# A hybrid Fourier and Hyena encoder layer on one core: another order of the Fourier phase, and first parts before second parts in the products

## The chip, the cores and the metric

The kernel runs on one core of one Trainium2 chip. The metric is the device time of one execution in microseconds (us), the median over several runs. A core has five engines with queues of their own: TensorE (PE, matrix products into PSUM), VectorE (DVE), ScalarE (ACT), GpSimd (POOL) and SyncE (SP, which only issues transfers here). ScalarE and GpSimd can issue transfers too. Each engine works through its instructions in the order in which the program holds them, and waits at the first whose inputs or buffers are not ready.

## The reference

Two sequences (called batches 0 and 1 here) of 1024 tokens by 1024 channels, in f32, go through the same layer:

```python
xn = rmsnorm(x, g_pre)
p = xn @ w_in
fv, fg, hv, hg, mg = split(p)                       # widths 1024, 1024, 3072, 1024, 2048
fz = fft over tokens and over groups of 256 channels of fv, real part
y_f = (fz * silu(fg)) @ w_fourier_out
v, x1, x2 = split(short_conv(hv, w_short))          # depthwise, width 3
kf = hyena_filters(...)                             # sin(w2 . sin(w1 . z)) @ w3, times exp decay, normalised, rfft
z = v
for n, gate in enumerate((x1, x2)):
    z = gate * long_conv(z, kf[:, n], hyena_d[n])   # FFT of length 2048, both directions
y_h = (z * silu(hg)) @ w_hyena_out
g_f, g_h = split(sigmoid(mg + b_merge))
out = (g_f * y_f + g_h * y_h) @ w_out
return x + rmsnorm(out, g_post)
```

## The kernel before

All large products run in a 32-bit format in which TensorE rounds its inputs (fp32r). To keep f32 accuracy each operand is split into a rounded first part h and a remainder l: `split` casts on ScalarE (L171) and subtracts on VectorE or GpSimd (L181). A product is then three matmuls, h by h, h by l and l by h; `mm3` issues them one after the other, and every matmul goes through one line (L194).

The work has four phases: `phase_fourier` (0 to about 226 us), `phase_main` (filters, input projections and long convolutions, to about 1720), `phase_gates` (to about 1924) and `phase_out`.

`phase_fourier` does for each batch the row norms, the scaled transposition of x, the projection to fv and the two-dimensional Fourier transform:

- `hidden(0)` makes the first layer of the filter network: two matmuls (phd), a range reduction in seven VectorE instructions each (`sin_of`), two Sin activations on ScalarE and a store. `hidden(1)` makes the second layer; it stands at the end of the phase.
- `norm(b)` loads the eight row tiles of x (128 tokens by 1024), squares each on ScalarE with a sum along the row (L320), computes the reciprocal roots in two groups of four tiles (`rstd`, L242 to L253, a chain of short VectorE instructions), and scales the identity by them into the diagonals dg (L325). For batch 1 the whole of it is pinned behind the last weight cast of half 1 (`behind`).
- `xtile(b, k)` multiplies blocks of x by the diagonals on TensorE (tpx), which transposes and normalises at once; ScalarE copies them out to xg (L344, two buffers, tag "xg", which the squares share); SP writes xg to DRAM (d_x, L345); VectorE and GpSimd form even and odd sums eo, which are split into eh and el. Token 512 is handled alone: two VectorE instructions of 128 by 2 elements for each k put its parts into `x5` (L173 and L181 in the profile).
- `weights(half, k)` loads 128 rows of the fv weights (wfv), forms sums wer and differences wor, and splits them into we and wo.
- `pfv` multiplies eh and el by the weights over eight k. In half (0, 0), six tiles are begun while the k come in, four in the four projection banks of PSUM (tag "mm") and two in banks with the tag "X". The sums of token 512 (p5, written pfx in the profile) are in an "X" bank.
- `fourier_half(b, half)` evicts the tiles as EE and OO, and runs the transform over tokens (`stage`: pse, pso, copied as sev, combined as sst, split as pp and qp) and over channels (pP, pQ), and stores fz. Its order is halves (0, 0), (0, 1), (1, 1), (1, 0).

The instructions are not in source order: a planner places them by its own costs when the kernel is built, subject to their dependencies. `tc.issue_after(i)` pins what is issued inside it behind instruction i, and `keep_in_program_order` ties one instruction. So a change of dependencies or pins also moves instructions that it does not name.

In the later phases `inproj` holds 128 by 512 weight parts h and l in two buffers each, makes them from a 256 KB load (wr: ScalarE casts wh, GpSimd subtracts wl) and multiplies them with all of xh and xl (pin). `forward` and `conv_back` are the transforms of the long convolution (pX, pT), `times` the products of the gates and of the output (pg, po), `project` those with w_fourier_out and w_hyena_out (pyf, pyh). All issue the three matmuls of a product in sequence:

```python
for n in range(2):
    for kk in range(4):
        k = 4 * q + kk
        s = slice(512 * n, 512 * n + 512)
        self.mm3(ps[:, s], (h[:, kk], l[:, kk]), (self.xh[k][:, s], self.xl[k][:, s]), k == 0, k == 7)
```

Of the kernel before, what the change touches and what calls it, by code (L numbers as in the profile page):

```python
# [16 lines left out]
P = 128  # L17
# [144 lines left out]
class K:  # L162
# [93 lines left out]
    def sin_of(self, y, k, out, src_ps, f, b):  # L256
# [14 lines left out]
        nc.scalar.activation(out, y, AF.Sin)  # L271

    def hidden(self, layer, px, pf):
# [14 lines left out]
        else:  # L288
# [5 lines left out]
            y, k = [[t[:, 0:512], t[:, 512:1024]] for t in (y, k)]  # L294
        for n in range(2):
            p = self.psum("mm", 4, "phd")
            nc.tensor.matmul(p, w, z[:, 512 * n:512 * n + 512], start=True, stop=True)
            self.sin_of(y[n], k[n], out[n], p, self.hfb[:, 2 * layer:2 * layer + 1],
                        self.hfb[:, 2 * layer + 1:2 * layer + 2])
        nc.sync.dma_start(self.d_h if layer else self.d_h1, h)  # L300


    def norm(self, b, px, pf):
# [3 lines left out]
        nc, a = self.nc, self.a  # L307
# [4 lines left out]
        for m in range(8):  # L312
# [4 lines left out]
            nc.sync.dma_start(x, a[f"x{b}"][m * P:(m + 1) * P, :])  # L317
            self.xs.append(x)
            sq = px.tile([P, D], F32, tag="xg", name="sq", bufs=2)
            nc.scalar.activation(sq, x, AF.Square, accum_out=ss[:, m:m + 1])  # L320
            if m % 4 == 3:
                q = slice(m - 3, m + 1)
                self.rstd(px, rs[:, q], ss[:, q], 4)
                for j in range(m - 3, m + 1):
                    nc.vector.tensor_scalar(dg[:, j], self.ident, rs[:, j:j + 1], None, op0=MUL)  # L325

    def xtile(self, b, k, px, fo):
# [11 lines left out]
        for n in range(2):  # L339
# [4 lines left out]
            nc.scalar.activation(xg[:, 512 * n:512 * n + 512], tp, AF.Copy, scale=self.gpre[:, k:k + 1])  # L344
        nc.sync.dma_start(self.d_x[b][k], xg[:, 0:L])  # L345
# [6 lines left out]
        x5 = fo["x5"][:, k]  # L352
        self.split(x5[:, b:b + 33:32], x5[:, 2 + b:35 + b:32], xg[:, 512:513].to_broadcast([P, 2]), "dve", "dve")
# [6 lines left out]
    def weights(self, pw, W, half, k, first):  # L360

        nc, a = self.nc, self.a
        w = pw.tile([P, 2, 2, 130], F32, tag="wfv", name="wfv", bufs=2)
        nc.sync.dma_start(w.rearrange("p a b c -> p (a b c)"), a["w_fv"][k * P:(k + 1) * P, half])
# [4 lines left out]
        for r, t in ((we, W[0]), (wo, W[1])):  # L369
            self.split(t[0][:, k], t[1][:, k], r.rearrange("p a b -> p (a b)"), "pool" if r is wo and not first else "dve", "act")  # L370
# [12 lines left out]
    def fourier_half(self, b, half, W, fo, px, pf, begun={}):  # L383
# [102 lines left out]
    def phase_fourier(self):  # L486
        tc, nc, a = self.tc, self.nc, self.a
        with ExitStack() as es:
# [7 lines left out]
            fo["x5"] = pc.tile([P, 8, 36], F32R, name="x5")  # L496
            fo["x5t"] = pc.tile([P, 260], F32R, name="x5t")
# [11 lines left out]
            for b in range(NB):  # L509
                fo["eh"] = pe.tile([P, 8, 2, 2, 256], F32R, tag="eh", name="eh")  # L510
                fo["el"] = pe.tile([P, 8, 2, 2, 256], F32R, tag="el", name="el")
                if b == 0:
                    self.hidden(0, px, pf)
                with tc.issue_after(behind.ins) if b else ExitStack():
                    self.norm(b, px, pf)
                begun = {}
                if b == 0:
                    W = self.open_weights(pw)
                    for e, m in [(0, 0), (0, 1), (0, 2), (0, 3), (1, 0), (1, 1)]:
                        begun[e, m] = self.psum("X", 2, "pfv1") if e else self.psum("mm", 4, "pfv0")  # L520
                for k in range(8):
                    if b == 0:
                        self.weights(pw, W, 0, k, True)
                    self.xtile(b, k, px, fo)
                    for (e, m), p in begun.items():
                        self.pfv(p, e, m, k, W, fo)
                for half in ((0, 1), (1, 0))[b]:
                    if b + half == 0:
# [936 lines left out]
```

## Time and profile before

| | |
|---|---|
| runs | 2443.44 to 2447.43 us, median 2446.82 |
| the profiled execution | 2449.26 us, its span 2447.1 us |
| granted TensorE clock, mean | 0.997 |
| TensorE | 2396.1 us busy, 13196 matmul records |
| VectorE, ScalarE, GpSimd | 1893.8, 1096.8 and 485.9 us busy |
| chain that ended last | PE 88%, DMA 5%, issue 3%, DVE 2% |

The names in the rows are those of the program with buffer numbers left out; `L194 PE MATMUL pin<-xh,wl` is the matmul of line 194 that writes pin from xh and wl. Behind a row of the groups stand the busy time, the mean duration of one in ns, the idle time of the engine just before them and what ended it. In a timeline row the start and the duration come first, and the idle time before it and its releaser stand in brackets. Matmuls overlap, so that the mean duration of one (392 ns for 512 columns) is longer than the distance between two.

### The profile page before, as it was taken

The page shows a single profiled execution, that of the slowest core. Times are in us where ns is not written, and L with a number is a line of the kernel's source. Part 1 is how long each engine was busy: PE and PEld are TensorE (multiplying, and loading weights), DVE is VectorE, ACT ScalarE, POOL GpSimd, SP SyncE. Part 2 cuts the span into 40 slices and gives each one's busy share as a digit, 9 for nine tenths or more (in the row PEclk, how much of TensorE's full clock was granted, in tenths as well). Part 3 has the DMA queues.
Part 4 walks back from the last instruction along what each step waited for, and adds up shares of the span by engine and source line. Part 5 has one row for each costly group of instructions (what it writes and reads, how often), then busy time and mean ns, then how long its engine had stood idle before and what let it go on. Part 6 is the DMA issues. An engine that isn't in the chain of part 4 may idle for free.

```text
span 2447.1 us, 36853 instructions
## 1 busy us (share of the span) xinstructions
PE 2396.1 (98%) x13196; PEld 2082.3 (85%) x13196; DVE 1893.8 (77%) x3405; ACT 1096.8 (45%) x2063; POOL 485.9 (20%) x516
## 2 busy tenths in 40 slices
PE   6999999999999999999999999999999999999998
PEld 5988888888888888888888888888788888888886
DVE  7687888888748999999989999766555455665677
ACT  5545677767633433334223333333344444544343
POOL 1341222222143433331000000112200111122111
PEclk9999999999999999999999999999999999999999
DMA  7545655555555555445434444335454567776543
GB/s 273 170 141 191 224 175 173 167 175 167 173 194 177 172 177 173 165 165 192 146 128 134 141 141 138 121 121 184 154 174 159 198 210 255 245 250 213 169 164 129
DMA packets 225151, 429.36 MB, mean 175 GB/s; under 512 B 23542, under 2 KB 87255, under 8 KB 224456
## 3 DMA queue, kind: packets, MB, share of 16 engines
q1 hardware_dynamic: 198444, 333.34, 41.1%
q0 software_dynamic: 26336, 93.65, 10.9%
q8 instruction: 104, 1.70, 0.3%
q14 instruction: 79, 0.65, 0.1%
q10 hardware_dynamic: 188, 0.02, 0.0%
HBM read 290.60 MB, written 136.31 MB: 174 GB/s over the span
## 4 chain that ended last, share of the span: by engine, by line
PE 88%; DMA 5%; issue 3%; DVE 2%; ACT 1%; POOL 1%; SPq 0%; DVEq 0%; POOLq 0%; ACTq 0%
PE pin L194 41%; PE pT L194 7%; PE pg L194 7%; PE pX L194 7%; PE po L194 6%; PE pyh L194 5%; PE pyf L194 5%; PE pXf L194 3%; PE pfv L194 2%; DMA wr<-in_w_fo 1%; PE pft L194 1%; PE tph L792 1%; DMA wr<-in_w_ho 1%; PE tpx L194 1%; DMA wfv<-in_w_fv 1%
## 5 line engine op out<-in xcount | busy, mean ns | idle before, releaser
L194 PE MATMUL pin<-xh,wl 128*128 128x512 f32 x1472 | 577.2, 392 | 2.6 <-POOL wl L181 2.6
L194 PE MATMUL pin<-xl,wh 128*128 128x512 f32 x1472 | 575.6, 391 | 2.4 <-DVE xl L181 2.4
L194 PE MATMUL pin<-xh,wh 128*128 128x512 f32 x1472 | 576.5, 392 | 0.7 <-DMA wh<-d_w 0.7
L181 POOL TENSOR_TENSOR wl<-wr,wh 128x512 fp32r<-128x512 f32 x136 | 240.3, 1768 | 1144.0 <-ACT wh L171 1105.9
L194 PEld LDWEIGHTS pin<-xh,wl 128*128 128x128 f32 x1472 | 277.1, 188 | 54.9 <-POOL wl L181 4.1
L194 PEld LDWEIGHTS pin<-xl,wh 128*128 128x128 f32 x1472 | 277.1, 188 | 54.3 <-DVE xl L181 3.2
L194 PEld LDWEIGHTS pin<-xh,wh 128*128 128x128 f32 x1472 | 277.1, 188 | 52.1 <-DMA wh<-d_w 1.1
L171 ACT CAST wh<-wr 128x512 fp32r<-128x512 f32 x264 | 162.8, 619 | 346.0 <-PE pin L194 136.8
L194 PE MATMUL pT<-cinv,yh 128*128 128x256 f32 x1024 | 193.1, 283 | 0.0
L194 PEld LDWEIGHTS pT<-cinv,yh 128*128 128x128 f32 x1024 | 164.0, 190 | 9.0
L181 DVE TENSOR_TENSOR t<-pX,k 128x1024 f32<-128x1024 f32 x128 | 155.9, 1218 | 10.9 <-PE pX L194 9.3
L194 PE MATMUL pX<-bh,cfwd 128*128 128x256 f32 x768 | 159.6, 286 | 0.0
L181 DVE TENSOR_TENSOR wl<-wr,wh 128x512 fp32r<-128x512 f32 x128 | 87.2, 687 | 93.5 <-ACT wh L171 93.2
L194 PE MATMUL pyf<-sf,wh 128*128 128x512 f32 x512 | 158.0, 390 | 0.9 <-ACT wh L171 0.9
L194 PE MATMUL pyh<-sh,wh 128*128 128x512 f32 x512 | 157.3, 389 | 0.0
L171 ACT CAST bh<-b 128x512 fp32r<-128x512 f32 x144 | 89.0, 620 | 126.7 <-DVE b L181 84.5
L194 PE MATMUL pT<-cinv,yl 128*128 128x256 f32 x512 | 144.9, 283 | 0.0
L171 ACT CAST yh<-y 128x512 fp32r<-128x512 f32 x128 | 79.2, 619 | 114.1 <-DVE y L181 91.3
L194 PEld LDWEIGHTS pX<-bh,cfwd 128*128 128x128 f32 x768 | 126.3, 190 | 2.5
L194 PEld LDWEIGHTS pyf<-sf,wh 128*128 128x128 f32 x512 | 96.0, 188 | 21.3 <-ACT wh L171 1.6
L194 PEld LDWEIGHTS pyh<-sh,wh 128*128 128x128 f32 x512 | 96.1, 188 | 19.9
L194 PE MATMUL pX<-bl,cfwd 128*128 128x256 f32 x384 | 109.6, 285 | 0.0
(354 smaller groups left out, 5262.7 us busy)
## 6 DMA issues: line engine op xcount, KB each, us to landing
k<-d_k SPq DMA_DIRECT2D x128, 512.0 KB, 4.0
wr<-in_w_in SPq DMA_DIRECT2D x136, 256.0 KB, 3.1
d_g<-gt SPq DMA_DIRECT2D x124, 256.0 KB, 2.6
d_k<-kt SPq DMA_DIRECT2D x128, 128.0 KB, 2.1
d_k<-kt SPq DMA_DIRECT2D x64, 256.0 KB, 2.3
wr<-in_w_fo POOLq DMA_DIRECT2D x64, 256.0 KB, 4.0
g<-d_g SPq DMA_DIRECT2D x64, 256.0 KB, 4.2
wr<-in_w_ho POOLq DMA_DIRECT2D x64, 256.0 KB, 3.7
```

Of the source, the lines that this page charges most:

```text
L171: self.rounded = nc.scalar.copy(h, src)
L181: return e.tensor_tensor(out, a, b, op=op)
L194: return self.nc.tensor.matmul(out, lhsT, rhs, start=start, stop=stop, skip_group_check=shared)
L792: nc.tensor.transpose(tp[:, q * P:(q + 1) * P], eo[:, e, q], self.ident)
```

## The change

The kernel after differs in these places:

1. **Batch 0's norms.** The loads of x alternate between SP's and ScalarE's queues. The weight rows of k = 0 are loaded after the fifth x tile and summed after the eighth square; their split and the weights of the other k are pinned behind the last diagonal. The reciprocal roots are taken in groups of tiles 0 to 3, 4 to 6 and 7.
2. **First filter layer.** `sin_of` returns its Sin as a function, `hidden` returns `end()`, and the two Sins and the store of layer 0 come after the last square.
3. **Batch 1's squares** are pinned one by one behind three marks: three behind the second odd tile of half (0, 0), three behind the weight cast of k = 1 of half (0, 1), two behind that of k = 5. The pin on the whole norm is gone.
4. **Token 512.** ScalarE copies its column of each k into `r5`; one split for each batch makes the parts. p5 is in a projection bank.
5. **Constants** seq, alt, chan, chx and vec are loaded once xg of k = 4 is there, not when the last reciprocal root is.
6. **Two more tiles** of the odd sums of half (0, 0) are begun in the "T" banks before the last k, with the 42 matmuls of the first seven k made up for there.
7. **Second filter layer** is issued ahead of the odd sums of half (1, 1), not at the end.
8. **The products** of the later phases take all matmuls with h as weights first, those with l after them; the number of matmuls stays.

The diff, cut to its core:

```diff
     def rstd(self, pool, out, ss, n):
-        m = pool.tile([P, n], F32, tag=f"rm{n}", name="rs_m", bufs=2)
-        t = pool.tile([P, n], F32, tag=f"rt{n}", name="rs_t", bufs=2)
+        m = pool.tile([P, max(n, 4)], F32, tag="rm", name="rs_m", bufs=2)[:, 0:n]
+        t = pool.tile([P, max(n, 4)], F32, tag="rt", name="rs_t", bufs=2)[:, 0:n]
...
+            if b == 0:
+                (nc.scalar if m % 2 else nc.sync).dma_start(x, a[f"x{b}"][m * P:(m + 1) * P, :])
+                if m == 4:
+                    raw = self.weight_rows(pw, 0, 0)
+        lo = 0
+        for m in range(8):
+            x = self.xs[m]
+            if b:
+                nc.sync.dma_start(x, a[f"x{b}"][m * P:(m + 1) * P, :])
             sq = px.tile([P, D], F32, tag="xg", name="sq", bufs=2)
-            nc.scalar.activation(sq, x, AF.Square, accum_out=ss[:, m:m + 1])
-            if m % 4 == 3:
+            with tc.issue_after(marks[(0, 0, 0, 1, 1, 1, 2, 2)[m]].ins) if b else ExitStack():
+                self.squared = nc.scalar.activation(sq, x, AF.Square, accum_out=ss[:, m:m + 1])
+            if m == 7 and b == 0:
+                raw = self.weight_sums(pw, raw, True)
+            if m in ((3, 6, 7), (3, 7))[b]:
...
+        if b == 0:
+            with tc.issue_after(self.scaled.ins):
+                self.weight_parts(W, 0, raw, True)
...
-        x5 = fo["x5"][:, k]
-        self.split(x5[:, b:b + 33:32], x5[:, 2 + b:35 + b:32], xg[:, 512:513].to_broadcast([P, 2]), "dve", "dve")
+        nc.scalar.copy(fo["r5"][:, k:k + 1], xg[:, 512:513])
...
+                if (b, half, e, m) == (1, 1, 1, 0):
+                    self.hidden(1, px, pf)()
...
+                if (e, m) == (1, 1):
+                    self.odd = self.rounded
...
-                        p5 = self.psum("X", 2, "pfx")[0:36, :260]
+                        p5 = self.psum("mm", 4, "pfx")[0:36, :260]
...
-                with tc.issue_after(behind.ins) if b else ExitStack():
-                    self.norm(b, px, pf)
+                self.norm(b, px, pf, pw, W, marks if b else None)
+                if b == 0:
+                    with tc.issue_after(self.squared.ins):
+                        end()
...
+                    if b == 0 and k:
+                        with tc.issue_after(self.scaled.ins):
+                            self.weights(pw, W, 0, k, True)
                     self.xtile(b, k, px, fo)
+                    if (b, k) == (0, 4):
                         nc.sync.dma_start(self.vec, a["c_vec"])
                         for t in ("seq", "chan"):
-                            nc.gpsimd.tensor_copy(fo[t][:, 0, 0:1], self.rs[:, 7:8])
+                            nc.gpsimd.tensor_copy(fo[t][:, 0, 0:1], self.xg[:, 0:1])
...
+                    if (b, k) == (0, 7):
+                        for m in (2, 3):
+                            begun[1, m] = self.psum("T", 2, "pfv1")
+                            for j in range(7):
+                                self.pfv(begun[1, m], 1, m, j, W, fo)
...
+                r5 = fo["r5"].unsqueeze(2).to_broadcast([P, 8, 2])
+                self.split(fo["x5"][:, :, b:b + 33:32], fo["x5"][:, :, 2 + b:35 + b:32], r5, "dve", "act")
...
+                            if b == 0 and k in (1, 5):
+                                marks.append(self.rounded)
...
-            self.mm3(X[:, i], tab(pr, 0), (h[:, 0:2], l[:, 0:2]), True, False)
-            self.mm3(X[:, i], tab(pr, 1), (h[:, 2:4], l[:, 2:4]), False, True)
+            for d, parts in ((h, (0, 1)), (l, (0,))):
+                for k in range(2):
+                    for t in parts:
+                        self.mm(X[:, i], tab(pr, k)[t], d[:, 2 * k:2 * k + 2], d is h and k + t == 0, d is l and k == 1)
...
+            for w, xs in ((h, (self.xh, self.xl)), (l, (self.xh,))):
+                for n in range(2):
                     s = slice(512 * n, 512 * n + 512)
-                    self.mm3(ps[:, s], (h[:, kk], l[:, kk]), (self.xh[k][:, s], self.xl[k][:, s]), k == 0, k == 7)
+                    for kk in range(4):
+                        k = 4 * q + kk
+                        for x in xs:
+                            self.mm(ps[:, s], w[:, kk], x[k][:, s], w is h and x is self.xh and k == 0, w is l and k == 7)
...
+        todo = [(0, k, j) for k in range(4) for j in range(2)] + [(1, k, 0) for k in range(4)]
+        for w, k, j in todo:
+            m = self.mm(p, A[w][:, k], B[k][j], first and w + k + j == 0, w + k == 4, True)
```

In `conv_back` and `project` the same is done with lists of the matmuls; `weights` is cut into `weight_rows`, `weight_sums` and `weight_parts`, which do the load, the sums and the splits as before.

More of the change, by code (lines that the diff above doesn't have):

```diff
@@ L270, in sin_of @@
         nc.vector.tensor_scalar(y, y, pi, -pi, op0=ALU.min, op1=ALU.max)
-        nc.scalar.activation(out, y, AF.Sin)
+        return lambda: nc.scalar.activation(out, y, AF.Sin)
     def hidden(self, layer, px, pf):
@@ L294, in hidden @@
             y, k = [[t[:, 0:512], t[:, 512:1024]] for t in (y, k)]
+        sins = []
         for n in range(2):
@@ L297, in hidden, with end, norm @@
             nc.tensor.matmul(p, w, z[:, 512 * n:512 * n + 512], start=True, stop=True)
[L298 to L307, printed above, removed]
+            sins.append(self.sin_of(y[n], k[n], out[n], p, self.hfb[:, 2 * layer:2 * layer + 1],
+                                    self.hfb[:, 2 * layer + 1:2 * layer + 2]))
+        def end():
+            for f in sins:
+                f()
+            nc.sync.dma_start(self.d_h if layer else self.d_h1, h)
+        return end
+    def norm(self, b, px, pf, pw, W, marks):
+        tc, nc, a = self.tc, self.nc, self.a
         ss = px.tile([P, 8], F32, tag="ss", name=f"ss{b}")
@@ L368, in weights, with weight_parts @@
         self.sub("dve" if first else "pool", wo, w[:, :, 0, 0:128], w[:, :, 1, 0:128])
-        for r, t in ((we, W[0]), (wo, W[1])):
-            self.split(t[0][:, k], t[1][:, k], r.rearrange("p a b -> p (a b)"), "pool" if r is wo and not first else "dve", "act")
+        return we, wo
+    def weight_parts(self, W, k, sums, first):
+        for i, (r, t) in enumerate(zip(sums, W)):
+            self.split(t[0][:, k], t[1][:, k], r.rearrange("p a b -> p (a b)"), "pool" if i and not first else "dve", "act")
     def mm3(self, out, L_, R_, start, stop):
@@ L816, in conv_back @@
             for r in range(2):
+                todo = []
                 for i, pr in enumerate(pairs):
[L818 removed]
                     o = IOFF[pr]
```

63 lines of the change are left out of this document (31 added, 32 removed).

## The prediction

> **What bounds the kernel now.** I read the page's busy line and its slices first, then a table of windows, then the matmul groups with the wait in front of each, and last the rows around each place where TensorE stood.
>
> ```profile
> PE 2396.1 (98%) x13196; PEld 2082.3 (85%) x13196; DVE 1893.8 (77%) x3405; ACT 1096.8 (45%) x2063; POOL 485.9 (20%) x516
> PE   6999999999999999999999999999999999999998
> ```
>
> TensorE is busy for 98% of the span. The matmul count of the program is the same after the change, so only stood time, or time at a lower clock, can be won. The windows say where that is (columns: length, then busy time and count of PE, PEld, DVE, ACT and POOL, then granted clock, DMA share, GB/s).
>
> ```profile
> 0.00:20.00 20.00, 5.86 (x12) 2.95 (x12) 11.72 (x37) 12.46 (x20) 2.68 (x10) 1.00 0.89 317
> 20.00:40.00 20.00, 12.95 (x83) 12.49 (x84) 15.90 (x49) 10.23 (x22) 1.67 (x7) 0.97 0.79 266
> 60.00:80.00 20.00, 20.00 (x167) 19.54 (x166) 11.41 (x30) 8.22 (x24) 8.62 (x10) 1.00 0.25 77
> 80.00:100.00 20.00, 17.46 (x130) 16.98 (x129) 15.06 (x50) 14.54 (x33) 5.28 (x9) 0.91 0.72 232
> 120.00:140.00 20.00, 16.29 (x134) 15.29 (x134) 18.40 (x37) 13.33 (x23) 9.54 (x13) 1.00 0.81 277
> 200.00:220.00 20.00, 15.90 (x129) 15.01 (x128) 11.03 (x25) 10.79 (x21) 2.15 (x4) 1.00 0.69 231
> 400.00:440.00 40.00, 40.00 (x226) 35.03 (x226) 33.17 (x79) 27.69 (x62) 7.62 (x6) 1.00 0.50 166
> 1700.00:1740.00 40.00, 37.53 (x165) 30.42 (x164) 24.81 (x21) 15.63 (x19) 14.44 (x8) 1.00 0.56 197
> ```
>
> In the main phase (400 to 440) TensorE does not stand at all. Nearly everything that can be won lies in the first 226 us (the Fourier phase), where TensorE is idle for 14.1 us in the first 20, 7.05 in the next, then 2.5, 3.7 and 4.1 in the three windows with the lowest busy time after that, and in a few places such as 1700 to 1740 (2.5 us). A change that works on these places alone cannot be worth more than some 20 us of 2449; one that spoils the order of the Fourier phase can cost as much.
>
> **The change, part by part.** The profiled execution took 2449.26 us (span 2447.1); the median of the three runs is 2446.82, 2.4 us less. I make the sum against 2449.26 and take 2.4 off at the end.
>
> *Head, batch 0's norms, weights and the late constants.*
>
> ```profile
> 17.08 2.08 PE L194 MATMUL tpx<-dg,x 128*128 128x128 f32 x8 [9.80 <-DMA wfv<-in_w_fv]
> 24.24 6.85 PE L194 MATMUL tpx<-dg,x 128*128 128x128 f32 x40 [5.09 <-DVE dg L325]
> 38.49 4.57 PE L194 MATMUL tpx<-dg,x 128*128 128x128 f32 x24 [2.62 <-ACT xg L344]
> 45.96 1.95 PE L194 MATMUL tpx<-dg,x 128*128 128x128 f32 x16
> ...
> 14.56 1.28 ACT L271 ACT_TABLE_LOAD   x1
> 15.85 0.63 ACT L271 ACTIVATE hd<-sq 128x512 f32<-128x512 f32 x1
> 18.98 1.04 ACT L320 ACTIVATE sq<-x 128x1024 f32<-128x1024 f32 x1
> ...
> 20.15 0.17 DVE L242 TENSOR_SCALAR rs_m<-ss 128x4 f32<-128x4 f32 x1 [1.52 <-ACT sq L320]
> 22.19 0.42 DVE L181 TENSOR_TENSOR wo<-wor,wo 128x256 fp32r<-128x256 f32 x1
> 22.52 0.16 DVE L253 SCALAR_TENSOR_TENSOR rs<-rs_t,rs 128x4 f32<-128x4 f32 x1
> 23.89 0.88 DVE L325 TENSOR_SCALAR dg<-ident,rs 128x128 f32<-128x128 f32 x4
> ```
>
> TensorE waits for the second set of scaled diagonals until 24.24. Before that, VectorE takes 3.74 us from rs_m (20.15) to dg (23.89), since sums and parts of weights (the wo of 22.19 is one) stand between the steps. The change pins the weights of k of 1 and more behind the last diagonal and runs groups of 3 and 1 interleaved; at the 0.2 us between the last three steps, which stand alone (22.52 to 23.89 is seven steps), eleven steps take 2.2. That is 1.5 us less; the one-column chain fills gaps and may add 0.5. On ScalarE the table load and two Sins, 1.28 + 2 x 0.63 = 2.5 us, go behind the squares, but the squares still wait for x, and the transfers are already 89% busy in that window, so alternating two issuing queues gets 0 from me and the squares end 0.8 earlier. Together -1.5 - 0.8 + 0.5 = -1.8 (bounds -2.6 to +0.5, the latter if the chains just add up). The first set of diagonals gets two weight sums (0.42 us each, as the wo above) ahead of it: nothing, since TensorE then waits for the second set anyway.
>
> ```profile
> 28.77 8.87 DMA d_x<-xg
> ...
> 24.41 0.53 POOL L532 DMA_DIRECT2D seq<-in_c_seq  x1 [0.18 <-POOL chan L531]
> ```
>
> The wait of 2.62 us at 38.49 is a buffer's: xg is free when the write of d_x has landed, and this took 8.87 us, beside the 2 MB of constants that POOL issued at 24.41. These now wait for xg of k = 4, some 10 us later, so the wait goes: -2.2 (bounds -2.6 to 0). The 24 matmuls behind it took 4.57 us, 190 ns each, where the 16 at 45.96 took 122: 24 x 68 = 1.6 us at a lower clock, of which I take -1.5 (0 to -1.6). What is late next: the writes of k = 4 to 7 beside the same constants. TensorE then has 42 matmuls of the two new half-finished tiles (at 20.00 / 167 = 0.12 us, 5 us of work) as cover; +0.5 (0 to +2.6, the wait over again). The new ScalarE copy and the lost 32 tiny VectorE instructions lie beside TensorE work here: 0. **Head: -5.0.**
>
> *Second batch's squares in three groups, 60 to 85 us.* Today the squares come after all weight casts of half 1; in the new order of ScalarE two stand ahead of the first cast, the third after two casts, the fourth and fifth ahead of the casts of k = 2, the last at k = 5 or 6.
>
> ```profile
> 82.68 1.05 ACT L320 ACTIVATE sq<-x 128x1024 f32<-128x1024 f32 x1
> 90.35 1.06 ACT L320 ACTIVATE sq<-x 128x1024 f32<-128x1024 f32 x1 [3.39 <-DMA x<-in_x]
> 91.66 0.38 ACT L431 COPY sev<-pse 128x258 f32<-128x258 f32 x1
> ...
> 92.13 0.60 PE L194 MATMUL pP<-pp,chan 128*128 128x258 f32 x3 [2.33 <-issue]
> ```
>
> Eight squares cost ScalarE 8 x 1.15 = 9.2 us with their sums read out; it has 20 - 8.22 = 11.8 us free in 60 to 80, so they fit, if x is there. Only three x buffers exist, so five loads wait for an earlier square, and the row at 90.35 shows what such a wait costs (3.39). Queued behind the waiting squares are the casts that half 1's matmuls need. From below 0 (all x there), from above one full wait of 3.39 for each of the five loads, 17 us. SP issues the loads earlier than the squares need them and the DMAs are only 25% busy here, which is nearer to the lower end; I take **+3.0**, two waits shortened by half.
>
> *89.5 us.* The rows above also show what goes: with the square of 90.35 waiting for x, the copy behind it (91.66) is late, and TensorE stands for 2.33 us at 92.13 and then runs at 0.91 of its clock over the window, 20 x 0.09 = 1.8 us. With the squares done earlier this goes: **-4.0** (bounds -4.1 to 0).
>
> By the Trainium skill (page "TensorE: Matmul & The Clock Gate", Part 1: The HAM clock gate) the clock falls only after an idle window of about 3.4 us. Here it fell after 2.62 and 2.33 us, so the measurement decides; by the page's figure these two places would return only their waits, and the sum would be 3.3 us smaller.
>
> *Batch 1's tiles, 110 to 160 us.* Token 512's values took a cast and a subtraction for each k on VectorE.
>
> ```profile
> 124.06 1.48 DVE L173 CAST x<-xg 128x2 fp32r<-128x2 f32 x1
> 125.57 1.45 DVE L181 TENSOR_TENSOR x<-xg,x 128x2 fp32r<-128x2 f32 x1
> ...
> 123.49 3.51 POOL L181 TENSOR_TENSOR eo<-xg 128x512 f32<-128x512 f32 x2 [0.91 <-ACT xg L344]
> ...
> 137.68 0.97 PE L194 MATMUL pso<-seq,oo 128*128 128x258 f32 x6 [1.26 <-DVE sst L181]
> ```
>
> Beside POOL's subtraction they took 1.5 us instead of 0.16, and TensorE stood for VectorE's sst soon after. One copy on ScalarE per k (under 0.4 us, the copy of 258 columns at 91.66) replaces them. Against that, p5 now holds one of the four projection banks through four tiles, and the second filter layer's 14 VectorE instructions (0.42 to 0.7 us, some 7.4 us) come ahead of the odd tiles' splits, where TensorE has less queued. **-0.5** (bounds -3.0, most of the 3.7 of the window, to +5.0, two thirds of those 7.4).
>
> *Hand-over to the main phase, 200 to 226 us.*
>
> ```profile
> 211.11 1.04 ACT L879 CAST hid<-hidr 128x1024 fp32r<-128x1024 f32 x1
> 212.79 1.28 ACT L642 ACT_TABLE_LOAD   x1
> 215.70 0.35 ACT L408 CAST x5t<-pfx 36x260 fp32r<-36x260 f32 x1
> ```
>
> TensorE is idle for 4.1 us in 200 to 220, in good part because the x5t cast stands behind the second layer's cast, a table load and four exponentials. In the new order it stands 20 instructions ahead of them. But one sev copy now stands behind two casts xh that wait for loads. **-3.0** (bounds -4.1 to +2.1, two such casts of 1.05 each).
>
> *First parts before second parts in the matmul order.*
>
> ```profile
> L194 PE MATMUL pin<-xh,wl 128*128 128x512 f32 x1472 | 577.2, 392 | 2.6 <-POOL wl L181 2.6
> L194 PE MATMUL pyh<-sh,wl 128*128 128x512 f32 x256 | 99.4, 390 | 1.2 <-DVE wl L181 1.2
> ...
> 1684.44 27.47 PE pin L194 x121
> ```
>
> Each matmul has a weight load of its own in both orders (the page counts 13196 of each), so I take the rate as unchanged. The second part of a weight is needed 16 matmuls (3.6 us at 27.47 / 121 = 0.227) later in the first and 8 later in the other; the waits of 2.6 and 1.2 go. xl is needed sooner, by 0.2 us. **-3.0** (bounds -3.8 to +0.7).
>
> *What no row shows.* Four pins and two moved banks make the planner lay out the first 226 us anew; each 20 us window of today with trouble loses 2.5 to 4 us, and one such new place is likely: **+2.0** (0 to +8, two of the worst).
>
> Sum: -5.0 + 3.0 - 4.0 - 0.5 - 3.0 - 3.0 + 2.0 = -10.5, so 2438.8 profiled and 2436.4 by the median; I say 2436.5.
>
> **Rivals.** (1) Slower: the squares starve TensorE. If five squares each wait 3.39 us for x ahead of half 1's casts, 17 us stand in place of the 3.0, and TensorE, out of other work, also runs cold for another 1.8: the sum becomes +5.3, 2452. It decides above 13.5 us of such waiting. For it: the 3.39 us wait exists today. Against it: DMA 25% busy, 11.8 us of free ScalarE.
> (2) The head's gain is eaten: the constants slow the later d_x writes as they slowed the earlier, x stays bound by transfers, and the squares' earlier loads do the same at 90 us. Head 0, the 89.5 place half, -3.5 in all: 2443.3. For it speaks the DMA share of 0.89 and 0.79 in the first windows.
> (3) VectorE becomes late in batch 1: the second layer's 7.4 us ahead of the odd tiles and the lost bank cost the upper bound, +5.0: 2442. VectorE is at 18.4 of 20 us in 120 to 140, which speaks for it.
> (4) The clock does not return with the waits (something else lowered it): 3.3 less, 2439.8. The page on TensorE named above would have it so; the two rows speak against.
>
> **How the numbers follow.** About 0.2% (4.9 us) is what a measurement of this kernel can tell from no change: faster is below 2441.9, slower above 2451.7. Chances: forecast 0.53, its own range 2428 to 2442; rival 1 0.19; rival 2 0.13; rival 3 0.09; rival 4 0.06. Faster: forecast and rival 4 and half of rival 3, 0.64; same: the other half and rival 2, 0.17; slower: rival 1, 0.19. The range leaves 0.1 on each side: from 2425 (every bound on the good side, no new wait: -6.8 + 0 - 4.1 - 3.0 - 4.1 - 3.8 = -21.8) to 2454 (rival 1 and a little over).
>
> **What would show it.** Right: the second group of tpx starts by 22.5, no wait for xg near 36 to 40, the groups pin and pyh with wl show no wait, the pP group none, and the x5t cast lies before the exponentials. Wrong: TensorE waits for we or wo between 60 and 85 of more than 5 us, clock below 0.95 there, or idle time in 100 to 200 above today's. The main phase from 250 to 1700 should keep its rate; a loss there would mean the matmul order costs something that I price at nothing.

## The result, and the profile after

The changed kernel took 2456.56 us (median of ten runs, 2447.99 to 2462.7); the kernel before took 2444.61 (ten runs, 2442.61 to 2450.08). The ratio is 1.0044 with a 95% interval of [1.0034, 1.0055]: slower by some 11 us, where I had forecast 10.5 us less. The profiled execution of the changed kernel took 2462.7 us (span 2460.9), the slowest of the ten.

The page of the changed kernel has TensorE as busy as before, and the windows show where it now stands (columns as in the prediction; the last two rows are the kernel before, where the prediction has no row).

```profile
PE 2403.3 (98%) x13196; PEld 2085.1 (85%) x13196; DVE 1907.8 (78%) x3384; ACT 1099.4 (45%) x2081; POOL 501.8 (20%) x516
```
```profile
20.00:40.00 20.00, 17.90 (x130) 16.73 (x129) 19.23 (x55) 15.64 (x34) 3.00 (x4) 1.00 0.64 228
60.00:80.00 20.00, 18.18 (x143) 16.80 (x143) 13.90 (x45) 16.36 (x41) 8.13 (x13) 1.00 0.77 248
80.00:100.00 20.00, 18.11 (x148) 17.29 (x147) 16.60 (x53) 8.31 (x22) 4.53 (x6) 1.00 0.36 104
120.00:140.00 20.00, 15.98 (x128) 14.83 (x126) 17.72 (x25) 13.11 (x29) 9.03 (x9) 1.00 0.83 287
140.00:160.00 20.00, 16.18 (x107) 15.06 (x106) 12.44 (x22) 7.45 (x15) 4.86 (x6) 0.83 0.34 133
200.00:220.00 20.00, 20.00 (x169) 19.84 (x169) 9.51 (x27) 7.27 (x15) 1.06 (x2) 1.00 0.61 220
1700.00:1740.00 40.00, 40.00 (x178) 33.14 (x177) 25.63 (x22) 16.07 (x21) 11.92 (x7) 1.00 0.61 207
2200.00:2240.00 40.00, 35.15 (x143) 28.47 (x143) 20.05 (x32) 17.30 (x30) 6.46 (x12) 0.91 0.69 232
...
140.00:160.00 20.00, 19.51 (x163) 19.30 (x163) 15.20 (x34) 8.48 (x19) 4.58 (x4) 1.00 0.21 80
2200.00:2240.00 40.00, 39.13 (x171) 31.75 (x170) 21.66 (x34) 20.13 (x35) 7.51 (x14) 1.00 0.65 220
```

The places that I had meant to clear are cleared: 20 to 40 us has 4.95 us more of TensorE's work, 200 to 220 and 1700 to 1740 have no idle time. But 140 to 160 now has 3.8 us of idle time at a clock of 0.83 (before: 0.5 us idle at 1.00), and 2200 to 2240 has 4.85 at 0.91 (before: 0.87 at 1.00). The groups of the changed kernel name the waits (behind the second bar: idle time before them, and what ended it; the last four rows are the kernel before):

```profile
L194 PE MATMUL pin<-xh,wl 128*128 128x512 f32 x1472 | 384.1, 392 | 0.0
L194 PE MATMUL pyh<-sh,wl 128*128 128x512 f32 x256 | 68.4, 389 | 0.0
L194 PE MATMUL pyf<-sf,wh 128*128 128x512 f32 x512 | 129.0, 395 | 9.4 <-ACT wh L171 9.4
L194 PE MATMUL pT<-cinv,yh 128*128 128x256 f32 x1024 | 164.8, 283 | 1.7 <-ACT T1s L894 1.0 <-ACT yh L171 0.6
L194 PE MATMUL pT<-cinv,yl 128*128 128x256 f32 x512 | 104.0, 285 | 1.1 <-DVE yl L181 1.1
L194 PE MATMUL pQ<-qp,chan 128*128 128x258 f32 (+1 forms) x48 | 10.5, 301 | 5.0 <-ACT qp L171 3.7 <-DVE qp L181 1.4
...
L194 PE MATMUL pyf<-sf,wh 128*128 128x512 f32 x512 | 158.0, 390 | 0.9 <-ACT wh L171 0.9
L194 PE MATMUL pT<-cinv,yh 128*128 128x256 f32 x1024 | 193.1, 283 | 0.0
L194 PE MATMUL pT<-cinv,yl 128*128 128x256 f32 x512 | 144.9, 283 | 0.0
L194 PE MATMUL pQ<-qp,chan 128*128 128x258 f32 (+1 forms) x48 | 10.0, 289 | 2.0 <-DVE fB L177 2.0
```

The waits for wl (2.6 and 1.2 before) are 0.0. New are those of pT (2.8) and of pQ for qp (5.0; before it waited 2.0 for something else), and that of pyf for wh grew from 0.9 to 9.4.

To compare kernels whose spans are shifted, I use one measure: the start of a matmul minus the sum of the undisturbed distances (from start to start) of all matmuls before it (226.6 ns for 512 columns, 119.6 for 256, 120.2 for 258, 110.5 for 128, the usual distances in these traces). That is how far TensorE is behind its work, in us, when so much work is done:

| work done, us | 40 | 80 | 120 | 200 | 280 | 1160 | 1700 | 2110 | 2300 |
|---|---|---|---|---|---|---|---|---|---|
| before | 29.9 | 34.5 | 39.9 | 49.0 | 49.7 | 57.2 | 62.6 | 64.1 | 67.1 |
| before, second profile (2444.39 us) | 29.1 | 30.6 | 36.1 | 45.2 | 46.5 | 54.5 | 59.8 | 61.4 | 62.2 |
| after | 25.0 | 30.5 | 44.8 | 48.1 | 52.0 | 62.1 | 65.4 | 72.6 | 80.5 |
| after, second profile (2455.3 us) | 26.2 | 32.5 | 46.2 | 49.6 | 50.9 | 66.4 | 70.5 | 71.2 | 73.1 |
| changed kernel, token 512's sums in the X bank (an experiment below) | 25.2 | 30.1 | 34.3 | 37.3 | 38.0 | 49.3 | 54.1 | 56.4 | 59.9 |
| the same, new order of the products in `inproj` alone (below) | 25.6 | 30.2 | 35.4 | 38.5 | 39.2 | 47.7 | 52.4 | 54.0 | 55.0 |

The head wins 3 to 5 us, all of it and more is lost between 80 and 120 us of work (14 us against 5.4), some is won again by 200; after that the kernel loses another 23 to 32 us, the kernel before 17 to 18.

### The profile page after: what moved, and what is told of

It reads as the page before. It is cut to its first block, busy times and chain, and to the rows that moved or that the text cites. A ratio compares the mean times of both kernels' runs of the same rounds, so it can differ in the third digit from the quotient of the medians.

```text
span 2460.9 us, 36910 instructions
## 1 busy us (share of the span) xinstructions
PE 2403.3 (98%) x13196; PEld 2085.1 (85%) x13196; DVE 1907.8 (78%) x3384; ACT 1099.4 (45%) x2081; POOL 501.8 (20%) x516
## 5 line engine op out<-in xcount | busy, mean ns | idle before, releaser
L194 PE MATMUL pin<-xh,wl 128*128 128x512 f32 x1472 | 384.1, 392 | 0.0
L194 PEld LDWEIGHTS pin<-xh,wh 128*128 128x128 f32 x1472 | 277.2, 188 | 52.6 <-DMA wh<-d_w 0.8
L194 PEld LDWEIGHTS pin<-xh,wl 128*128 128x128 f32 x1472 | 270.2, 189 | 50.6
L194 PE MATMUL pT<-cinv,yh 128*128 128x256 f32 x1024 | 164.8, 283 | 1.7 <-ACT T1s L894 1.0
L194 PEld LDWEIGHTS pT<-cinv,yh 128*128 128x128 f32 x1024 | 145.3, 190 | 9.1 <-ACT yh L171 1.6
L194 PE MATMUL pyf<-sf,wh 128*128 128x512 f32 x512 | 129.0, 395 | 9.4 <-ACT wh L171 9.4
L194 PE MATMUL pX<-bh,cfwd 128*128 128x256 f32 x768 | 131.0, 287 | 0.0
L194 PE MATMUL pyh<-sh,wh 128*128 128x512 f32 x512 | 126.6, 389 | 0.7 <-ACT wh L171 0.7
L194 PEld LDWEIGHTS pX<-bh,cfwd 128*128 128x128 f32 x768 | 110.3, 190 | 3.9
L181 DVE TENSOR_TENSOR bl<-b,bh 128x512 fp32r<-128x512 f32 x144 | 105.5, 735 | 7.7 <-ACT bh L171 6.7
L194 PE MATMUL pT<-cinv,yl 128*128 128x256 f32 x512 | 104.0, 285 | 1.1 <-DVE yl L181 1.1
```

Source lines behind the costliest of these rows:

```text
L181: return e.tensor_tensor(out, a, b, op=op)
L194: return self.nc.tensor.matmul(out, lhsT, rhs, start=start, stop=stop, skip_group_check=shared)
```

## The experiments

All ratios are against the kernel before, run on the same chip beside each kernel; 0.1% is 2.4 us. In the head of each experiment stand the ratio, its 95% interval and the median.

**The order of the products undone (1.0017 [1.0008, 1.0025], 2448.85), and alone on the kernel before (1.0023 [1.0014, 1.0032], 2449.54).** The first is, in `forward`, and alike in the other four functions, the diff below; the second has part 8 in all five and nothing else of the change. (In `forward` the weights are the transform tables, so there the order goes by the parts of the other operand.)

```diff
-            for d, parts in ((h, (0, 1)), (l, (0,))):
-                for k in range(2):
-                    for t in parts:
-                        self.mm(X[:, i], tab(pr, k)[t], d[:, 2 * k:2 * k + 2], d is h and k + t == 0, d is l and k == 1)
+            self.mm3(X[:, i], tab(pr, 0), (h[:, 0:2], l[:, 0:2]), True, False)
+            self.mm3(X[:, i], tab(pr, 1), (h[:, 2:4], l[:, 2:4]), False, True)
...
```

> The changed kernel with the three matmuls of every product in the old order again (part 8 undone in all five functions). Theory P (the product order brought the loss: in the profile after, 10 us more are lost from 2120 to 2240 and 3 to 4 from 280 to 320 and 900 to 1160): about 10 us less than the changed kernel, 2445 to 2448. Theory F (the Fourier phase brought it, 7 us more lost from 120 to 160, and the product order is worth the 3 us that I forecast): 2458 to 2461, with the waits of pin and pyh for wl back.

> The kernel before with part 8 alone. Theory P: 8 to 12 us more than before, 2453 to 2457, lost in the last 400 us. Theory F: 3 us less, 2441 to 2442.

Undoing the order takes 0.27% off the changed kernel (6.6 us), and adding it to the kernel before costs 0.23% (5.6 us). Theory P was right in the sign, with two thirds of the size; what is left of the change without part 8 still costs 0.17%, so neither theory alone holds. The price of the order is not a fixed one: with the X bank it is 0.18%, and with the old handling of token 512 nothing that can be told (both below).

**The old order in `project` alone (1.0027 [1.0017, 1.0037], 2451.6).**

```diff
                     for kk in range(4):
-                        for x in S[4 * q + kk]:
-                            self.mm(ps, h[:, kk], x, 4 * q + kk == 0 and x is S[0][0], False)
-                    for kk in range(4):
-                        self.mm(ps, l[:, kk], S[4 * q + kk][0], False, 4 * q + kk == 7)
+                        k = 4 * q + kk
+                        self.mm3(ps, (h[:, kk], l[:, kk]), S[k], k == 0, k == 7)
```

> The changed kernel with the old order in project alone (pyf and pyh). If theory P holds and project is its place: 6 to 10 us less than the changed kernel, no wait of pyf for wh above 1.5 us. If the loss there comes from elsewhere (a later start of the stage, or chance): within 2 us of the changed kernel. Theory F: no change or 1 us more.

0.17% less (4.2 us) than the changed kernel, less than the 6 us that I expected, and the wait of pyf for wh falls from 9.4 to 0.8 us. The same step on top of the X bank (below) won 0.14%.

**Token 512 as before (1.0043 [1.003, 1.0056], 2456.45).**

```diff
-        nc.scalar.copy(fo["r5"][:, k:k + 1], xg[:, 512:513])
+        x5 = fo["x5"][:, k]
+        self.split(x5[:, b:b + 33:32], x5[:, 2 + b:35 + b:32], xg[:, 512:513].to_broadcast([P, 2]), "dve", "dve")
...
-                        p5 = self.psum("mm", 4, "pfx")[0:36, :260]
+                        p5 = self.psum("X", 2, "pfx")[0:36, :260]
```

> The changed kernel with token 512 handled as before (two VectorE instructions a tile, sums in the X bank). If the waits of 110 to 160 us come from the lost projection bank or from the eight ScalarE copies: 4 to 8 us less than the changed kernel. If they come from tiles that now arrive earlier, beside the stages of the first batch: within 2 us, or 1 to 3 us more, since the 1.5 us VectorE instructions beside GpSimd are back.

No change in time, but not for the reason given: TensorE is 30.0 us behind at 40 us of work (25.0 with the change), 41.6 at 120 (44.8) and 52.6 at 200 (48.1). The gain of the head is gone, the loss between 80 and 120 us of work is 7 us instead of 14, and a new one of 10 us stands at the hand-over. Its timeline, TensorE and then ScalarE:

```profile
59.55 0.50 PE L194 MATMUL pfv<-wo,eh 128*128 128x256 f32 x2 [3.05 <-ACT xg L365]
218.88 1.50 PE L194 MATMUL pse<-seq,ex 128*34 128x258 f32 x6 [3.64 <-ACT sev L465]
```
```profile
58.81 1.26 ACT L365 ACTIVATE xg<-tpx,gpre 128x512 f32<-128x512 f32 x2 [5.08 <-DMA d_x<-xg]
...
215.14 0.42 ACT L670 ACTIVATE dec<-dec 128x256 f32<-128x256 f32 x1 [2.38 <-DMA dec<-in_filt_decay]
215.57 1.28 ACT L690 ACT_TABLE_LOAD   x1
216.87 1.70 ACT L690 ACTIVATE ex<-dec,vec 128x256 f32<-128x256 f32 x4
218.47 0.35 ACT L465 COPY sev<-pse 128x258 f32<-128x258 f32 x1
```

At 58.81 the copy to xg waits until a write of d_x has left its buffer; at 218.47 sev stands behind an activation that waits 2.38 us for a load, a table load and four exponentials. So the two halves of part 4 had to be taken apart.

**The four corners of part 4.** Each half of the diff above alone: the sums in the X bank with the new parts (0.9998 [0.9989, 1.0007], 2443.11); the sums in the projection bank with the old parts (1.0054 [1.0042, 1.0066], 2457.24).

> The changed kernel with token 512's sums in the X bank again, its parts made the new way. If the bank moved the loss (from the hand-over at 200 to 226 into the window of 110 to 160): the window 120 to 160 loses 5 to 7 us less, the hand-over 4 to 8 more, and the time stays within 2 us. If the eight ScalarE copies in their place did it: the window stays as it is.

> The changed kernel with token 512's parts made by two VectorE instructions a tile again, its sums in the projection bank as in the changed kernel. The fourth corner of a square (bank old or new, parts old or new; the other three took 2456, 2443 and 2456). If the new bank costs 13 us whatever the parts: 2465 or more. If bank and old parts hit the same wait once: 2454 to 2459.

| ratio | X bank | projection bank |
|---|---|---|
| two VectorE instructions a tile | 1.0043 | 1.0054 |
| ScalarE copy, one split | 0.9998 | 1.0044 |

With the new parts the bank alone costs 0.46%, 11 us: as much as the whole change lost. The old parts cost that much by themselves (0.9998 to 1.0043), and with them the bank costs only 0.11%, which is within the spread of the runs. So the old parts with the projection bank end in the lower range that I expected, but not because they hit the same wait: that kernel is already 31.8 us behind at 40 us of work. In the kernel with the X bank and the new parts the window did lose less, as the first expectation had it, but the hand-over did not lose more, and the time went down by 11 us instead of staying. In the kernel with the X bank the pQ wait is gone, and so is the low clock:

```profile
L194 PE MATMUL pQ<-qp,chan 128*128 128x258 f32 (+1 forms) x48 | 9.6, 284 | 0.0
```
```profile
120.00:140.00 20.00, 18.29 (x152) 17.51 (x151) 19.29 (x31) 14.84 (x29) 9.03 (x9) 1.00 0.61 222
140.00:160.00 20.00, 20.00 (x157) 18.50 (x156) 17.34 (x43) 5.72 (x14) 1.23 (x3) 1.00 0.14 54
```

In the changed kernel (TensorE, ScalarE, VectorE, of one stretch) the wait looks so:

```profile
141.00 0.51 PE L194 MATMUL pfv<-we,eh 128*128 128x260 f32 x2 [0.75 <-ACT eh L171]
143.73 0.39 PE L194 MATMUL pQ<-qp,chan 128*128 128x258 f32 x1 [2.21 <-ACT qp L171]
146.39 0.80 PE L194 MATMUL pQ<-qp,chan 128*128 128x258 f32 x2 [0.85 <-DVE qp L181]
```
```profile
139.91 1.05 ACT L171 CAST eh<-eo 128x1024 fp32r<-128x1024 f32 x1 [1.46 <-DVE eo L181]
140.95 1.27 ACT L365 ACTIVATE xg<-tpx,gpre 128x512 f32<-128x512 f32 x2
142.11 1.04 ACT L171 CAST eh<-eo 128x1024 fp32r<-128x1024 f32 x1
143.04 0.63 ACT L171 CAST qp<-sst 128x514 fp32r<-128x514 f32 x1
```
```profile
137.86 2.56 DVE L181 TENSOR_TENSOR eo<-xg 128x512 f32<-128x512 f32 x2
```

TensorE has nothing else to do there: it is down to one to three matmuls of pfv at a time between the steps of the channel transform. In the kernel with the X bank the sums of token 512 run as a lump of 16 behind the tiles, tpx of batch 1 begins at 105.2 us and ends at 131; in the changed kernel the sums lie between the tiles, one or four at a time, tpx begins at 108.8 and ends at 137. I read it so: a bank that is held from the first sum to the last leaves three of four for the tiles, and for tpx of batch 1, which by the code takes its banks from the same four; the planner orders what follows around it. That the bank is the cause is shown, by which of these steps isn't. By my estimate up to 3.4 of the 11 us are the low clock (20 x 0.17).

**Where the bank costs (half (0, 1) alone: 1.0009 [0.9999, 1.0019], 2446.15; the other halves alone: 1.0022 [1.0011, 1.0032], 2450.26).**

```diff
-                        p5 = self.psum("mm", 4, "pfx")[0:36, :260]
+                        p5 = (self.psum("mm", 4, "pfx") if (b, half) == (0, 1) else self.psum("X", 2, "pfx"))[0:36, :260]
```

> The changed kernel with token 512's sums in a projection bank in half (0, 1) alone, in the X bank in the other halves. If the bank costs in half (0, 1), where the profile of the changed kernel has the sums between the tiles and loses 13 us from 120 to 160: 2454 to 2457, as the changed kernel. If it costs in the other halves: 2443, as with the old bank everywhere.

> The changed kernel with the sums in the X bank in half (0, 1) alone, in a projection bank in the other halves: the other way round, 2443 if half (0, 1) is the place, 2454 to 2457 if not.

Neither expectation held. Against the X bank everywhere (0.9998), the other halves cost 0.24%, and the projection bank everywhere costs 0.46%, so it is not one place; the 0.11% of half (0, 1) alone is too small for the runs to tell from nothing. The profiles say the same: at 200 us of work the first kernel is 4 us further behind than the kernel with the X bank, the second 6 and the changed kernel 11. They also part the two steps of my reading. In the first kernel the sums lie between the tiles of half (0, 1) and tpx begins at 109.1 and ends at 136.5 us, as late as in the changed kernel, yet pQ waits 0.4 us in all and 140 to 160 us runs without idle time at 1.00. So the late tpx alone brings neither the pQ wait nor the low clock. In the second kernel the wait sits in half (1, 1), for a remainder el that VectorE makes late:

```profile
138.82 0.39 PE L194 MATMUL pfv<-we,el 128*128 128x260 f32 x1 [2.09 <-DVE el L181]
```

**Old products and old token 512 (1.0043 [1.0031, 1.0055], 2455.37).** Both diffs above together.

> The changed kernel with the old order of the products and the old handling of token 512: what is left are the head, the pins of the second batch's squares and the place of the second filter layer. If these are worth what the traces of the head show (5 us at 40 us) and nothing is given back: 2438 to 2441. If the gain is given back in the next 100 us: 2444 to 2449.

Slower than either expectation. The head alone is not worth anything with the old parts of token 512: TensorE is 32.4 us behind at 40 us of work, more than before the change. And the old products, worth 6.6 us on the changed kernel, are worth nothing here: the same kernel with the new ones stands at 1.0043 too.

**The X bank with all products old (0.998 [0.9972, 0.9989], 2440.3), with the new order in `inproj` alone (0.9979 [0.9971, 0.9988], 2438.6), with the old order in `project` alone (0.9984 [0.9975, 0.9992], 2441.15).** All have

```diff
-                        p5 = self.psum("mm", 4, "pfx")[0:36, :260]
+                        p5 = self.psum("X", 2, "pfx")[0:36, :260]
```

and the old text of `forward`, `conv_back`, `times`, `project` and `inproj`, of the first four, or of `project`.

> The changed kernel with token 512's sums in the X bank and all products in the old order. If the two losses add up: the Fourier phase of the kernel with the old bank alone (37 us behind the work at 200 us of work, 45 to 49 before), the later phases as before (15 us more up to the end): 2434 to 2438, faster than both kernels. If the later phases just lose elsewhere what the first wins: 2442 to 2446.

> As the kernel with the old bank, with the new order of the products in inproj alone. If the waits of pT for yl and yh between 900 and 1160 come from the new order in forward and conv_back: no such wait, the two waits of pin for wl at 1710 and 1730 gone, 2 to 3 us less than with all products old. If they come from inproj's new order (it moves where the planner puts pin between the transforms): 3 us lost there as in the changed kernel, and no gain.

> As the kernel with the old bank, with project alone in the old order. If project's new order brings the loss between 2110 and 2240, as the 5 us between the changed kernel and the same with the old project say: 3 to 5 us less than the kernel with the old bank, 2438 to 2440. If that loss hangs on when the phase begins: within 1.5 us of it.

All three beat the kernel before. The first lies between its two expectations. The second is 0.21% (5 us) faster than it and 18 us by the medians faster than the changed kernel. The new order in `inproj` alone is worth nothing that these runs can tell from the old one (0.9979 and 0.998), so the 2 to 3 us that I expected of it do not show. The order in `project` costs 0.14% here too, at the lower end of what I expected. The waits of pT (3.9 us against 0.7) belong to the new order in `forward`, `conv_back` or `times`, hardly to that in `inproj`; first the third kernel, then the second:

```profile
L194 PE MATMUL pT<-cinv,yh 128*128 128x256 f32 x1024 | 165.0, 284 | 2.1 <-ACT T1s L894 1.0 <-ACT yh L171 1.0
L194 PE MATMUL pT<-cinv,yl 128*128 128x256 f32 x512 | 104.2, 285 | 1.8 <-DVE yl L181 1.8
```
```profile
L194 PE MATMUL pT<-cinv,yh 128*128 128x256 f32 x1024 | 192.8, 283 | 0.2 <-ACT yh L171 0.2
L194 PE MATMUL pT<-cinv,yl 128*128 128x256 f32 x512 | 145.5, 284 | 0.5 <-DVE yl L181 0.5
L194 PE MATMUL pyf<-sf,wh 128*128 128x512 f32 x512 | 157.7, 389 | 0.0
```

**On the fastest kernel, the old pin of the squares (1.0007 [0.9998, 1.0015], 2446.82) and the old place of the second filter layer (0.9991 [0.9982, 0.9999], 2443.56).** First the one, then the other:

```diff
-            with tc.issue_after(marks[(0, 0, 0, 1, 1, 1, 2, 2)[m]].ins) if b else ExitStack():
+            with ExitStack():
...
-                self.norm(b, px, pf, pw, W, marks if b else None)
+                with tc.issue_after(behind.ins) if b else ExitStack():
+                    self.norm(b, px, pf, pw, W, None)
...
-                            if b == 0 and k in (1, 5):
-                                marks.append(self.rounded)
+                        behind = self.rounded
```
```diff
-                if (b, half, e, m) == (1, 1, 1, 0):
-                    self.hidden(1, px, pf)()
...
+                    if (b, half) == (1, 1):
+                        self.hidden(1, px, pf)()
```

> The fastest kernel so far (old bank, new order in inproj alone, 2438.6) with the old pin: all of batch 1's squares behind the last weight cast of half 1. By my sum (squares in groups +3.0, the wait at 89.5 gone -4.0) 1 us more. If the squares' casts starve TensorE as rival 1 has it, more than that comes back: 2 to 5 us less. If the earlier norms are what lets batch 1's tiles begin sooner: 5 us more or over.

> The fastest kernel so far with the second filter layer at the end of the phase again. If its place is what clears the hand-over to the main phase (the cast of hid there waits for the layer's store and load): 4 to 6 us more, with a wait for x5t or sev at 200 to 215. If the new place only fills VectorE ahead of the odd tiles: 0 to 2 us less.

The pins in groups are worth 0.28% (7 us), the place of the second layer 0.12% (3 us, below the 4 to 6 expected). At 60 to 100 us the old pin costs nothing: TensorE is 29.1 us behind at 80 us of work, 30.2 with the new one. Its cost comes at the hand-over, where it loses 9.4 us between 160 and 200 us of work (2.9 with the new pins): x5t and xh stand on ScalarE behind two instructions that wait for loads. TensorE, then ScalarE:

```profile
205.77 0.51 PE L194 MATMUL pse<-alt,x5t 128*128 128x258 f32 x2 [1.43 <-DVE x5t L181]
211.62 0.80 PE L194 MATMUL pin<-xh,wh 128*128 128x512 f32 x1 [4.62 <-ACT xh L171]
```
```profile
202.96 1.05 ACT L927 CAST hid<-hidr 128x1024 fp32r<-128x1024 f32 x1 [3.00 <-DMA hidr<-d_h]
207.20 0.42 ACT L668 ACTIVATE dec<-dec 128x256 f32<-128x256 f32 x1 [2.62 <-DMA dec<-in_filt_decay]
```

With the old place of the second layer TensorE waits 3.06 us for x5t there.

**Both kernels once more (2444.39 and 2455.3).**

> The kernel before, unchanged, profiled a second time: how far its profile of 2449.26 us, which lies above the median of its other runs (2445), differs from another by place. If the extra 4 us sit in one place: the last 400 us, where the transfers are the busiest. Else spread over the places where TensorE waits.

> The changed kernel, unchanged, profiled a second time. Its first profile (2462.7) was 6 us above the median. If the loss from 2110 to 2240 is a collision of transfers that depends on the run, most of the 6 us are gone there, and the losses from 100 to 160 (7 us more than before) and 900 to 1160 (3 more) stay within 1 us, being set by the order of the instructions.

For the kernel before, the difference of 5 us does not lie in the last 400 us as I expected, but mostly at 80 to 100 us: the wait of 2.33 us and the low clock are not in the second profile.

```profile
80.00:100.00 20.00, 18.98 (x155) 18.48 (x155) 15.94 (x56) 14.77 (x34) 4.36 (x8) 1.00 0.78 248
```

For the changed kernel, the loss of 15 us from 1700 on in the first profile is 3 in the second (the last columns of the table above), with the wait of pyf for wh at 1.6 us instead of 9.4; the loss at 80 to 120 us of work is the same in both (14.3 and 13.7), and from 280 to 1160 it is 5 us more (15.5 against 10.1). So the loss at 80 to 120 comes with the order of the instructions, while those of the later phases move with the run.

## Why the prediction was wrong

Two terms of the sum failed, both with the wrong sign: batch 1's tiles (-0.5), where the moved bank costs 11 us beside the new parts, and the order of the products (-3.0), which costs 6.6 us on the changed kernel. With both undone the kernel is 5 us faster than the one before (0.998), and the other terms of the sum, together -7.0, are near that. This nearness is in part luck: the terms of the squares and of 89.5 us are off by more than the difference, as said below.

- **Head, -5.0: right in size.** 4.9 us by the first pair of profiles, 2.9 by the second. The second tpx group starts by 21.6 and there is no wait for xg at 38. But I priced the ScalarE copies and the lost VectorE instructions at 0, as beside other work, and that was wrong. In the second profile of the kernel before, the wait for xg is there (3.25 us at 38.73), but not the lower clock, so the 1.5 us of clock in this term are not certain either. The gain hangs on the copies: at 40 us of work it is gone in all three kernels with the old parts (30.0, 31.8, 32.4 against 25.0).
- **Squares, +3.0: right at the place** (waits for we of 2.7 us from 60 to 90), but the sum left out what earlier norms do 120 us later. By the runs on the fastest kernel the grouped pins gain 7 us. Rival 1 did not happen.
- **89.5 us, -4.0: an accident of one profile.** The second profile of the kernel before does not have it. I took a term of full size from one execution that was over 4 us above the median of ten, and took only 2.4 off at the end.
- **Batch 1's tiles, -0.5: the step that failed most.** With the new parts in place the bank costs 11 us, beyond my bound of +5.0. I had priced a bank as a resource whose lack delays a split; what it did was to change the order: the sums of token 512 lie in among the tiles of halves (0, 1) and (1, 1), tpx is put off by 4 to 6 us, and TensorE is left with nothing beside the channel transform. Which of these costs how much stays open, but half (0, 1) alone, with the late tpx, costs at most a part. The 11 us hold only beside the new parts: part 4 as a whole, undone, gives nothing back (1.0043), since the old parts lose as much at other places. Rival 3 came nearest: it has the lost bank in it, but at +5.0 together with the second layer, which gains 3 us.
- **Hand-over, -3.0: about right** (4.3 us less between 160 and 200 us of work, of which 3 are given back by 280 in the first pair of profiles and none in the second), and by more kinds of moves than I had named.
- **First parts first, -3.0: wrong in sign, +6.6 on the changed kernel, +5.6 on the kernel before, +4.4 with the X bank, 0 with the old token 512.** The waits for wl went as forecast (3.8 us). (They are needed 14 and 6 matmuls later, not 16 and 8, since wl was the third matmul of a product before.) In their place came waits of pT (2.8 and 4.8 us in the two profiles of the changed kernel) and of pyf for wh. The latter are 1.6 to 9.4 us in all eight profiles with the new order in `project` (changed kernel 9.4 and 1.6, X bank 4.5, part 8 alone 3.2), and 0.0 to 1.2 in all ten with the old (kernel before 0.9 and 0.0, old `project` alone 0.8). So the order in `project` does bring this wait. The chain of the changed kernel shows one of them:

```profile
2206.55 9.12 DMA t1l<-d_t
2215.69 7.72 DMA g<-d_g
2224.12 0.61 ACT wh L171
2224.78 1.22 PE pyf L194 x2
```

  The cast wh stands on ScalarE behind the sigmoid of g, g is issued by SP when a 1 MB load has landed, and TensorE waits 4.85 us. The kernel before waits at the same place, 0.9 us, there too after a slow load of g (10.45 us in its chain). Why the new order makes it longer is not settled: the same number of matmuls lies between two weights in both orders, and the planner also moved casts and loads there; no kernel here kept its order and changed only the matmuls. The sign that I had named for this came too: from 280 to 1700 us of work the changed kernel loses 13.4 and 19.6 us in its two profiles, the kernel before 12.9 and 13.3.
- **Unknown places, +2.0: the right kind of term, but too small.** The 14 us between 80 and 120 us of work, against 5.4 before, are more than its upper bound of 8 allows; they are the same loss as the bank's, since with the X bank it is 4.2.
- **The clock.** At the two places that I had named the waits are gone and the clock is 1.00 (20 to 40 and 80 to 100 us), so rival 4 did not happen. A wait by itself does not settle the clock, though. After 2.21 us at 143.73, with 0.75 ahead of it, the window of 140 to 160 ran at 0.83, so again the clock fell after less idle time than the 3.4 us of the Trainium skill ("TensorE: Matmul & The Clock Gate", Part 1: The HAM clock gate). But after 3.25 us at 38.73 in the second profile of the kernel before, and after 3.20 at 2206.88 in the kernel with the X bank, the clock of the windows stays 1.00. And in the first 20 us the column is no witness: in the kernel before it says 1.00 there, while 8 tpx take 2.08 us at 17.08, more than 16 of them (1.95) at 45.96.

## What to carry to other kernels

Where a planner lays out the program, an edit that shifts a buffer or an order by one step is priced by what the planner then puts beside it: look for the stretch in which TensorE has a single chain of work left, and ask what the edit does to the order there. Take terms of a sum from two executions, not one, when the kernel's runs spread as widely as the terms. And test the parts of a bundled change apart, and say beside which others a part was priced: here one line cost as much as the whole lost, a second part half as much, and what was left without them was 5 us faster than the kernel before; but with the old parts of token 512 neither of the two changed the time.

## What the runs showed that I had not expected

Eight pairs of VectorE instructions of 0.16 us decided whether 5 to 7 us at 40 us of work were won. They lie between eo and el on a VectorE that is busy 19.2 of 20 us in 20 to 40, and moving them moves the planner's order; which of the two did it, the runs do not tell. And two costs of the same size did not add up: X bank with old parts, and projection bank with new parts, each cost 11 us, both together 14, and the runs hardly tell the 14 from the 11.
